# Expert layer: query products in small steps between the sums, the first head's first 128 tokens alone, the first closing norm later

## The chip, the cores and the metric

The kernel runs on one core of one Trainium2 chip. The metric is device time in microseconds (us) of one execution; less is better.

## The reference, cut to what matters

The reference is a whole network on 256 tokens of width 1024: two mixing layers, a layer with a recurrence and attention, and last a layer of experts. Only the expert layer is touched. For each token it makes queries for 8 heads, scores them against two sets of 128 keys, takes the 16 best pairs, fetches for each pair one row of `u` and one row of `v` from tables of 16,384 rows, and adds up 128 rows of `v` per token, each with a coefficient:

```python
def one_chunk(xt):
    q = (xt @ w_q).reshape(BLOCK, PEER_HEADS, PEER_QDIM)
    s1 = jnp.einsum('chd,nd->chn', q[..., :half], keys1).astype(jnp.float32)
    s2 = jnp.einsum('chd,nd->chn', q[..., half:], keys2).astype(jnp.float32)
    t1, i1 = lax.top_k(s1, PEER_TOPK)
    t2, i2 = lax.top_k(s2, PEER_TOPK)
...
    ts, sel = lax.top_k(cand, PEER_TOPK)
    idx = jnp.take_along_axis(cidx, sel, axis=-1)
    g = jax.nn.softmax(ts, axis=-1)
    act = jax.nn.gelu(jnp.einsum('chkd,cd->chk', u[idx], xt))
    coef = (g * act.astype(jnp.float32)).astype(xt.dtype)
    return jnp.einsum('chk,chkd->cd', coef, v[idx])
```

The sum is added to the residual `h`, and a closing RMS norm with a gain gives the output.

## The kernel before

The last stage, `layer_d` (L1382), works in 16 units: 2 tiles of 128 tokens (`tt`) by 8 heads (`h`), the 8 heads of tile 0 first. A unit has 16 gathers. A gather (L1511) is one indirect DMA that POOL issues: for each of 128 tokens one row of `uv`, 8 KB with `u` and `v` side by side, 1 MB in all, into one of 9 slots of a ring (`RING`). Two other users take a slot of the ring: `sq`, the squares for the norm, ahead of the first gather, and `o`, the output tile of a closing norm.

What a unit needs before its gathers:

- `queries(h)` (L1426): for all 256 tokens, 16 matmuls of 128x128 weights by 256 columns (8 pieces `k` of the model width, 2 halves `f`) into one PSUM bank `pq`. An fp32 matmul has two records in the trace, called pieces here.
- `scores(h)` (L1438): ACT copies `pq` to `q`, 4 matmuls of 128 columns (`psc`) multiply with the keys, and ACT copies the scores of tile 0 (`sc0`, two buffers) and of tile 1 (`later`).
- `select(tt, h)` (L1465): on DVE, the 16 best of each key set and then of their pairs (MAX8, FIND_INDEX8 and MATCH_REPLACE8 in the trace), and the row numbers `idx` (L1500), for which POOL waits. It is a generator, so that its steps can be written between experts.

What happens to a gathered row is `expert` (L1514): a product sum on DVE with the normed token rows `xtok` (L1518, `dots`), GELU, coefficient and a diagonal matrix `dg` on ACT (L1521 to L1524), and two matmuls of 512 columns on PE that add `dg` times `v` to `acc[tt]` in PSUM (L1526). Experts run 7 gathers behind (`AHEAD`), and a gather waits until the expert 9 before it has left its slot.

`residual(tt)` (L1408) puts the residual into `acc[tt]` with 8 small matmuls, `token_rows(tt)` (L1450) makes `xtok` from it on DVE, and `close(tt)` (L1530) does the closing norm: a square with sum on ACT (L1534), mean on DVE (L1535), the power -1/2 on POOL (`fy`, L1536), two multiplies on DVE (L1539) and two DMAs of 256 KB from SP (L1540).

The order on each engine is made by a scheduler from the order in which the code stands and from which inputs are ready; each engine then runs its list strictly in order. `tc.issue_after(last)` ties the instructions of a block on one engine behind a given instruction of that engine. Before the change it is used for the steps of `select` only, with the `dots` instruction of the last expert. `queries(i + 1)` and `scores(i + 1)` stand at the head of unit `i`, untied. In front of the gathers stands, for head 0, the product of all 256 tokens and then `rms_cols` (`pst`), which sums the squares `sq` that ACT and POOL prepare.

Of the kernel before, what the change touches and what calls it, by code (L numbers as in the profile page):

```python
# [11 lines left out]
F32 = mybir.dt.float32  # L12
# [4 lines left out]
AF = mybir.ActivationFunctionType  # L17
# [4 lines left out]
P = 128  # L22
D = 1024
KT = D // P
T = 256
# [105 lines left out]
def rms_cols(g, pool, pst, squares, tiles, tag):  # L131

    nc = g.nc
    for i, sq in enumerate(squares):
        token_sums(nc, pst, g.ones, sq, tiles, i == 0, i == len(squares) - 1)
    m, y = (pool.tile([P, len(tiles)], F32, tag=tag + u, name=u) for u in ("ms", "rs"))
    whole = sum(nt == P for _, nt in tiles)
    nc.vector.tensor_scalar(m[:, 0:whole], pst[:, 0:whole], 1.0 / D, 1e-6, ALU.mult, ALU.add)
    for j in range(whole, len(tiles)):
        nt = tiles[j][1]  # L140
        nc.vector.memset(m[:, j:j + 1], 1.0)
        nc.vector.tensor_scalar(m[0:nt, j:j + 1], pst[0:nt, j:j + 1], 1.0 / D, 1e-6, ALU.mult, ALU.add)
    nc.gpsimd.tensor_tensor(y, m, g.mhalf[:, 0:1].to_broadcast([P, len(tiles)]), ALU.pow)
    return y
# [1215 lines left out]
NK = 128  # L1360
PH = 8
TOPK = 16
# [19 lines left out]
def layer_d(g, a, ht, wpools):  # L1382
    tc, nc, g.ahead = g.tc, g.nc, 0
    V, S, G, PE = nc.vector, nc.scalar, nc.gpsimd, nc.tensor
    xt = ht[:, :, META:]
    with ExitStack() as ctx:
# [19 lines left out]
        acc = [pv.tile([P, D], F32, name=f"acc{tt}") for tt in range(2)]  # L1406

        def residual(tt):  # L1408

            for k in range(KT):  # L1410
                PE.matmul(acc[tt][:, k * P:(k + 1) * P], xt[:, k, tt * P:(tt + 1) * P], g.ident, start=(k % 4 == 0),
                          stop=False, skip_group_check=True)

        pf = ctx.enter_context(tc.tile_pool(name="d_f", bufs=1, reuse_waits="tile"))
        later = pf.tile([P, PH, 2, NK], F32, name="sc1")
        sc = {}
        xg = pf.tile([P, KT, T], F32, name="xg")
# [5 lines left out]
            if k:  # L1423
                G.tensor_add(sq[:, k:k + 2, :], sq[:, k:k + 2, :], sq[:, k - 2:k, :])

        def queries(h):  # L1426
            w = g.wq[h]
            p = ps.tile([P, 512], F32, tag="mm", name="pq")
            for k in range(KT):
                for f in range(2):  # L1430
                    PE.matmul(p[:, f * T:(f + 1) * T], w[k // 4][:, k % 4, f * P:(f + 1) * P], xg[:, k, :],  # L1431
                              start=(k == f == 0), stop=(k == KT - 1), skip_group_check=True)
            return p

        ahead = [queries(0)]
        rs = rms_cols(g, px, ps.tile([P, 512], F32, tag="sm", name="pst"), [sq[:, k, :] for k in (KT - 2, KT - 1)], TILES, "d")

        def scores(h):  # L1438
            q = pf.tile([P, 2, T], F32, tag="q", name="q", bufs=2)
            S.activation(q, ahead.pop(0).rearrange("p (f t) -> p f t", f=2), AF.Copy)  # L1440
            p = ps.tile([P, 512], F32, tag="sm", name="psc")
            for tt in range(2):
                for f in range(2):
                    o = (tt * 2 + f) * NK
                    PE.matmul(p[:, o:o + NK], q[:, f, tt * P:(tt + 1) * P], kys[:, f, :], start=True, stop=True)
            sc[0, h], sc[1, h] = pf.tile([P, 2, NK], F32, tag="sc0", name="sc0", bufs=2), later[:, h]
            for tt in range(2):
                S.activation(sc[tt, h].rearrange("p f n -> p (f n)"), p[:, tt * 2 * NK:(tt + 1) * 2 * NK], AF.Copy)

        def token_rows(tt):  # L1450

            for j in range(2):
                js = slice(j * 512, (j + 1) * 512)
                V.tensor_mul(xtok[tt][:, js], acc[tt][:, js], gain["norm2_b"][:, js])
# [54 lines left out]
        def gather(b, s):  # L1509
            r = ring.tile([P, 2 * D], F32, tag="uv", name="uv")  # L1510
            G.indirect_dma_start(r, None, a["uv"], bass.IndirectOffsetOnAxis(ap=b.idx[:, s:s + 1], axis=0))  # L1511
            return r

        def expert(b, s, r):  # L1514

            junk = pk.tile([P, D], F32, tag="junk", name="junk", bufs=1)
            d = dots[:, b.tt, b.h, s:s + 1]
            done = V.tensor_tensor_reduce(out=junk, in0=r[:, 0:D], in1=xtok[b.tt], scale=1.0, scalar=0.0,  # L1518
                                          op0=ALU.mult, op1=ALU.add, accum_out=d)
            gl, cf = (pk.tile([P, 1], F32, tag=u, name=u, bufs=4) for u in ("gl", "cf"))  # L1520
            S.activation(gl, d, AF.Gelu_apprx_tanh, scale=rs[:, b.tt:b.tt + 1])  # L1521
            S.activation(cf, gl, AF.Copy, scale=b.e[:, s:s + 1])  # L1522
            dg = pk.tile([P, P], F32, tag="dg", name="dg", bufs=3)
            S.activation(dg, g.ident, AF.Copy, scale=cf)  # L1524
            for j in range(2):
                PE.matmul(acc[b.tt][:, j * 512:(j + 1) * 512], dg, r[:, D + j * 512:D + (j + 1) * 512], start=False,  # L1526
                          stop=(b.h == PH - 1 and s == TOPK - 1), skip_group_check=True)
            return done.ins

        def close(tt):  # L1530

# [11 lines left out]
        scores(0)  # L1543
        waiting, last = [], None
        for i, (tt, h) in enumerate(order):
            b = Ctx()
            b.tt, b.h = tt, h
            if i == 0:
                for _ in select(tt, h, b):
                    pass  # L1550
                residual(0)
                token_rows(0)
            else:
                for _ in nxt[1]:
                    pass
                b = nxt[0]
            if i + 1 < len(order):
                n = Ctx()
                n.tt, n.h = order[i + 1]
                if i + 1 < PH:  # L1560
                    ahead.append(queries(i + 1))
                    scores(i + 1)
                nxt = n, select(n.tt, n.h, n)
                if i == 2:
                    residual(1)
                    token_rows(1)
            for s in range(TOPK):
                waiting.append((b, s, gather(b, s)))
                if s % 3 == 0 and nxt:
                    with tc.issue_after(last) if last else nullcontext():  # L1570
                        next(nxt[1], None)
                if len(waiting) > AHEAD:
                    last = expert(*waiting.pop(0))
            if i == PH:
                close(0)
        for w in waiting:
            expert(*w)
# [180 lines left out]
```

## Time and profile before

| | us |
|---|---|
| median of 3 runs | 1391.04 |
| lowest and highest | 1388.09 and 1393.73 |
| the profiled execution | 1389.13 |
| its span (first to last instruction) | 1387.2 |
| outside the span | 1.93 |

PE was granted 0.982 of full speed over the span. The chain that ended last, followed back from the end, is 36% PE, 32% DMA, 11% DVE, 10% issue time, 5% ACT and 4% POOL; the DMA part is almost all gathers (30%). Times in the rows further down are us from the start of the span. In the table of stretches, the columns are busy time of each engine with its count of instructions, the granted clock, the busy share of the 16 DMA engines, and what they moved. The expert layer fills the second half: its first gather is issued at 712.73 us.

### The profile page before, as it was taken

To read this page: it belongs to the slowest core of one execution; us is meant where nothing else is said; L and a number is where in the kernel's file an instruction comes from. 1 tells how busy PE (TensorE), PEld (TensorE's weight loads), DVE (VectorE), ACT (ScalarE), POOL (GpSimd) and SP (SyncE) were. 2 spreads that over 40 slices of the span, in tenths; PEclk is the share of its full clock that TensorE was granted. 3 is DMA by queue.
4 is the path that set the end of the run, shared out by engine and by line. 5 is a ranking of instruction groups with operands and counts; after the bars stand their busy time and mean duration, and the time that the engine had idled before them with its cause. 6 is when DMAs were issued, how large, how long until landed. Compare 5 with 4: busy or idle time off the path is not lost.

```text
span 1387.2 us, 18959 instructions
## 1 busy us (share of the span) xinstructions
PE 1232.9 (89%) x6566; PEld 848.1 (61%) x6566; DVE 884.4 (64%) x2103; ACT 664.2 (48%) x1554; POOL 392.3 (28%) x387
## 2 busy tenths in 40 slices
PE   8999997999999899999999998778887778777776
PEld 7778786899998899999976653223222222222222
DVE  6276626676666878666666656766676666666644
ACT  1254522556564686555333455544444444444433
POOL 1001046211114300000043345344443444344430
PEclk9999999999999999999999999999999899999999
DMA  6411311354426354335769999999999899999996
GB/s 233 162 63 61 100 32 39 114 176 131 136 94 204 115 182 142 105 127 188 229 242 420 387 350 422 419 420 420 421 419 419 348 420 420 420 420 420 420 420 248
DMA packets 69727, 364.23 MB, mean 263 GB/s; under 512 B 8752, under 2 KB 14320, under 8 KB 36864
## 3 DMA queue, kind: packets, MB, share of 16 engines
q0 software_dynamic: 36864, 268.45, 47.2%
q1 hardware_dynamic: 32768, 94.56, 21.0%
q8 instruction: 53, 0.87, 0.3%
q14 instruction: 42, 0.34, 0.1%
HBM read 361.94 MB, written 1.05 MB: 262 GB/s over the span
## 4 chain that ended last, share of the span: by engine, by line
PE 36%; DMA 32%; DVE 11%; issue 10%; ACT 5%; POOL 4%; POOLq 0%; SPq 0%; DVEq 0%; ACTq 0%
DMA uv<-in_uv,idx 30%; PE pj L105 5%; PE c_mm L105 5%; PE acc L1526 4%; DVE junk L1518 3%; DVE wl L69 2%; POOL uv L1511 2%; PE pt L313 2%; PE pf L313 2%; PE por L828 2%; PE pf L105 1%; PE pp L614 1%; PE m_mm L105 1%; PE por L105 1%; PE pS L940 1%
## 5 line engine op out<-in xcount | busy, mean ns | idle before, releaser
L1526 PE MATMUL acc<-uv,dg 128*128 128x512 f32 x1024 | 503.6, 622 | 117.7 <-ACT dg L1524 114.1
L1518 DVE CUSTOM_DVE_ANT_0 junk<-uv,xtok 128x1024 f32<-128x1024 f32 x256 | 312.8, 1222 | 208.3 <-DMA uv<-in_uv,idx 207.8
L1526 PEld LDWEIGHTS acc<-uv,dg 128*128 128x128 f32 x1024 | 181.8, 192 | 421.6 <-ACT dg L1524 275.8
L1511 POOL DMA_INDIRECT uv<-in_uv,idx x256 | 273.8, 1070 | 366.0 <-PE acc L1526 265.9
L1521 ACT ACTIVATE gl<-dots,rs 128x1 f32<-128x1 f32 x256 | 75.1, 293 | 296.8 <-DVE dots L1518 296.5
L68 ACT ACTIVATE wh<-raw 128x1024 fp32r<-128x1024 f32 (+2 forms) x124 | 125.8, 1028 | 78.0 <-PE c_mm L105 24.7
L69 DVE TENSOR_TENSOR wl<-raw,wh 128x1024 fp32r<-128x1024 f32 (+3 forms) x115 | 138.2, 1215 | 27.4 <-ACT wh L68 27.0
L1524 ACT ACTIVATE dg<-ident,cf 128x128 f32<-128x128 f32 x256 | 102.5, 400 | 17.2 <-PE acc L1526 9.5
L1522 ACT ACTIVATE cf<-gl,ex 128x1 f32<-128x1 f32 x256 | 75.1, 293 | 7.8
L105 PE MATMUL c_mm<-xgh,wl 128*128 128x256 f32 (+2 forms) x232 | 69.2, 298 | 1.7 <-DVE wl L69 1.7
L105 PE MATMUL c_mm<-xgh,wh 128*128 128x256 f32 (+2 forms) x232 | 68.2, 294 | 1.6 <-DVE xp L1097 1.3
L105 PE MATMUL pj<-wh,xih 128*128 128x256 f32 x240 | 69.4, 289 | 0.0
L105 PE MATMUL pj<-wh,xil 128*128 128x256 f32 x240 | 68.8, 286 | 0.4 <-DVE xil L806 0.4
L105 PE MATMUL pj<-wl,xih 128*128 128x256 f32 x240 | 67.6, 282 | 0.3 <-DVE wl L69 0.3
L105 PE MATMUL c_mm<-xgl,wh 128*128 128x256 f32 (+2 forms) x232 | 67.6, 291 | 0.0
L313 PE MATMUL pt<-wp,xm 128*128 128x256 f32 x256 | 62.3, 389 | 0.0
L1431 PE MATMUL pq<-xg,wq 128*128 128x256 f32 x256 | 60.2, 379 | 0.0
L1431 PEld LDWEIGHTS pq<-xg,wq 128*128 128x128 f32 x256 | 48.0, 190 | 15.6 <-issue 10.5
L313 PEld LDWEIGHTS pt<-wp,xm 128*128 128x128 f32 x256 | 46.3, 190 | 7.3 <-issue 0.3
L105 PEld LDWEIGHTS pj<-wh,xih 128*128 128x128 f32 x240 | 45.2, 188 | 3.7 <-issue 3.3
L105 PEld LDWEIGHTS c_mm<-xgh,wl 128*128 128x128 f32 (+1 forms) x232 | 44.1, 190 | 3.2 <-DVE wl L69 2.9
L105 PEld LDWEIGHTS c_mm<-xgh,wh 128*128 128x128 f32 (+1 forms) x232 | 44.1, 190 | 2.5 <-issue 1.5
(449 smaller groups left out, 2331.8 us busy)
## 6 DMA issues: line engine op xcount, KB each, us to landing
wq<-in_wd_q SPq DMA_DIRECT2D x16, 512.0 KB, 6.9
wp<-in_wa_k SPq DMA_DIRECT2D x8, 512.0 KB, 9.5
raw<-in_wa_o SPq DMA_DIRECT2D x8, 512.0 KB, 3.9
wp<-in_wa_r SPq DMA_DIRECT2D x8, 512.0 KB, 4.8
wp<-in_wa_v SPq DMA_DIRECT2D x8, 512.0 KB, 4.4
wp<-in_wa_g SPq DMA_DIRECT2D x8, 512.0 KB, 4.3
raw<-in_wb_k SPq DMA_DIRECT2D x8, 512.0 KB, 3.9
raw<-in_wb_q SPq DMA_DIRECT2D x8, 512.0 KB, 4.0
```

The source lines that it names most:

```text
L68: nc.scalar.activation(xh, x, AF.Copy)
L69: return (engine or nc.vector).tensor_sub(xl, x, xh.bitcast(F32)).ins
L105: last = nc.tensor.matmul(out, s, m, start=(k == n == 0), stop=(k == kt - 1 and n == len(ops) - 1))
L313: PE.matmul(out, s, m, start=(k == 0), stop=(k == KT - 1))
L828: last = nc.tensor.matmul(out, m, v, start=(k == n == 0 and fresh), stop=(k == KT - 1 and n == 2), skip_group_check=True)
L1431: PE.matmul(p[:, f * T:(f + 1) * T], w[k // 4][:, k % 4, f * P:(f + 1) * P], xg[:, k, :], start=(k == f == 0), stop=(k == KT - 1), skip_gr ...
L1511: G.indirect_dma_start(r, None, a["uv"], bass.IndirectOffsetOnAxis(ap=b.idx[:, s:s + 1], axis=0))
L1518: done = V.tensor_tensor_reduce(out=junk, in0=r[:, 0:D], in1=xtok[b.tt], scale=1.0, scalar=0.0, op0=ALU.mult, op1=ALU.add, accum_out=d)
L1521: S.activation(gl, d, AF.Gelu_apprx_tanh, scale=rs[:, b.tt:b.tt + 1])
L1522: S.activation(cf, gl, AF.Copy, scale=b.e[:, s:s + 1])
L1524: S.activation(dg, g.ident, AF.Copy, scale=cf)
L1526: PE.matmul(acc[b.tt][:, j * 512:(j + 1) * 512], dg, r[:, D + j * 512:D + (j + 1) * 512], start=False, stop=(b.h == PH - 1 and s == TOPK - ...
```

## The change

`queries` becomes a generator that yields after each of the 8 pieces `k`, and can take half of the tokens. Its steps, 2 matmuls each, are asked for at every second gather, two heads ahead of the unit that needs them, and tied on PE behind the matmuls of the expert before (`behind(1)`; `expert` now returns these too). `scores` follows at the end of the unit. Ahead of the first gather only the queries and scores of the first 128 tokens of head 0 are made; head 1, the residual, the token rows and the other 128 tokens of head 0 come after `select` of unit 0. `sc0` has three buffers in place of two. `residual(1)` stands ahead of the gathers of unit 1 (before: unit 2). `close(0)` stands at the end of unit 11 (before: unit 8).

```diff
-        def queries(h):
-            w = g.wq[h]
-            p = ps.tile([P, 512], F32, tag="mm", name="pq")
+        def queries(h, to, tiles=slice(0, T)):
+
+            w, n = g.wq[h], tiles.stop - tiles.start
+            to.append(ps.tile([P, 512], F32, tag="mm", name="pq"))
+            p = to[-1]
             for k in range(KT):
                 for f in range(2):
...
-            return p
-
-        ahead = [queries(0)]
+                yield
+
+        ahead = []
+        for _ in queries(0, ahead, slice(0, P)):
+            pass
...
-            return done.ins
+            return done.ins, summed.ins
...
+        def behind(i):
+
+            return tc.issue_after(last[i]) if last else nullcontext()
+
+        scores(0, (0,))
+        for _ in units[0].steps:
+            pass
+        for h, tiles in ((1, slice(0, T)), (0, slice(P, T))):
+            for _ in queries(h, ahead, tiles):
+                pass
+            if h:
                 residual(0)
                 token_rows(0)
...
+                scores(1)
+        scores(0, (1,))
+        for i, b in enumerate(units):
+            then = units[i + 1] if i + 1 < len(units) else None
+            asked = queries(i + 2, ahead) if i + 2 < PH else iter(())
+            for _ in b.steps:
+                pass
+            if i == 1:
+                residual(1)
+                token_rows(1)
             for s in range(TOPK):
                 waiting.append((b, s, gather(b, s)))
-                if s % 3 == 0 and nxt:
-                    with tc.issue_after(last) if last else nullcontext():
-                        next(nxt[1], None)
+                if s % 3 == 0 and then:
+                    with behind(0):
+                        next(then.steps, None)
+                if s % 2:
+                    with behind(1):
+                        next(asked, None)
                 if len(waiting) > AHEAD:
                     last = expert(*waiting.pop(0))
-            if i == PH:
+            if i + 2 < PH:
+                for _ in asked:
+                    pass
+                with behind(1):
+                    scores(i + 2)
+            if i == PH + 3:
                 close(0)
```

What the change makes of the engines' lists, at three places. First PE ahead of the first gather, before (`pq` are queries, `pst` the sums of squares, `acc` from `ident` the residual, `psc` scores):

```order
L1431 MATMUL pq<-xg,wq 128x256 x16
L127 MATMUL pst<-ones,sq 128x1 x4
L1411 MATMUL acc_7240<-ident,ht 128x128 x3
L1445 MATMUL psc<-kys,q 128x128 x4
L1411 MATMUL acc_7240<-ident,ht 128x128 x5
L1431 MATMUL pq<-xg,wq 128x256 x18
```

and after:

```order
L1433 MATMUL pq<-xg,wq 128x128 x16
L127 MATMUL pst<-ones,sq 128x1 x4
L1433 MATMUL pq<-xg,wq 128x256
L1450 MATMUL psc<-kys,q 128x128 x2
L1433 MATMUL pq<-xg,wq 128x256 x15
L1411 MATMUL acc_7240<-ident,ht 128x128 x8
L1450 MATMUL psc<-kys,q 128x128 x4
```

The first queries have half the columns, two score matmuls follow the sums of squares after one other matmul, and the residual has moved behind them. On DVE, in the same place, the list before has the token rows inside the first selection:

```order
L1483 CAST ivf<-iv 128x32
L1454 TENSOR_TENSOR xtok_7237<-acc_7240,norm_b 128x512
L1458 MAX ts<-cand 128x8
L1454 TENSOR_TENSOR xtok_7237<-acc_7240,norm_b 128x512
L1459 MAX_INDEX se<-ts,cand 128x8
```

and after, behind the row numbers of unit 0:

```order
L1501 TENSOR_TENSOR eq<-eq,ivf 128x512
L1503 TENSOR_REDUCE ix<-eq 128x32
L1505 SCALAR_TENSOR_TENSOR idx<-ix 128x16
L1459 TENSOR_TENSOR xtok_7237<-acc_7240,norm_b 128x512 x2
L1463 MAX tv<-sc_7381 128x8 x2
```

Both multiplies of `token_rows(0)` now stand after `idx`. Second, PE among the experts of units 1 and 2 (two `acc` matmuls are one expert), before:

```order
L1526 MATMUL acc_7240<-uv,dg 128x512 x2
L1431 MATMUL pq<-xg,wq 128x256 x3
L1526 MATMUL acc_7240<-uv,dg 128x512 x2
L1431 MATMUL pq<-xg,wq 128x256 x4
L1526 MATMUL acc_7240<-uv,dg 128x512 x2
L1431 MATMUL pq<-xg,wq 128x256 x3
```

and after:

```order
L1450 MATMUL psc<-kys,q 128x128 x4
L1531 MATMUL acc_7240<-uv,dg 128x512 x2
L1433 MATMUL pq<-xg,wq 128x256 x2
L1531 MATMUL acc_7240<-uv,dg 128x512 x4
L1433 MATMUL pq<-xg,wq 128x256 x2
L1531 MATMUL acc_7240<-uv,dg 128x512 x4
```

Before, the last query matmul stands ahead of expert 30 (of 256, counted from 0), with three or four between two experts; after, it is two for every two experts, up to expert 88. Third, POOL around the first closing norm, as one piece of the difference:

```order
-L1511 DMA uv<-in_uv,idx 128x2048 x144
-L1536 TENSOR_TENSOR fy_9678<-fm_9677,mhalf 128x1
-L1511 DMA uv<-in_uv,idx 128x2048 x112
-L1536 TENSOR_TENSOR fy_11409<-fm_11408,mhalf 128x1
+L1516 DMA uv<-in_uv,idx 128x2048 x192
+L1541 TENSOR_TENSOR fy_10427<-fm_10426,mhalf 128x1
+L1516 DMA uv<-in_uv,idx 128x2048 x64
+L1541 TENSOR_TENSOR fy_11429<-fm_11428,mhalf 128x1
```

and ACT there, after the change (the `gl` ahead of the square is the one of expert 189; before the change it is the one of expert 141):

```order
L1526 ACTIVATE gl<-dots,rs 128x1
L1539 ACTIVATE o,fss_10425<-acc_7240 128x1024
L1527 ACTIVATE cf<-gl,ex 128x1
L1529 ACTIVATE dg<-ident,cf 128x128
L1526 ACTIVATE gl<-dots,rs 128x1
```

The closing norm has moved by 48 gathers; `fy` still stands directly behind the last gather of a unit on POOL, and the square on ACT behind the GELU of the expert two before that gather.

## Rows read from the trace of the kernel before

**Rows 1.** The page's first line: span and instructions.

```profile
span 1387.2 us, 18959 instructions
```

**Rows 2.** Stretches of the expert layer: busy by engine, clock, DMA share, GB/s.

```profile
720.00:780.00 60.00, 57.72 (x216) 36.68 (x215) 40.66 (x109) 28.22 (x78) 23.00 (x22) 1.00 1.01 418
780.00:832.00 52.00, 51.31 (x162) 29.51 (x163) 30.38 (x84) 24.18 (x75) 21.77 (x21) 1.00 0.96 352
832.00:1070.00 238.00, 190.48 (x385) 67.74 (x384) 160.54 (x428) 113.52 (x318) 104.93 (x97) 0.98 1.01 420
1070.00:1100.00 30.00, 20.31 (x40) 7.27 (x40) 18.54 (x56) 10.82 (x33) 10.68 (x10) 0.94 0.84 335
```

**Rows 3.** Gathers, answer on line L1511: time from issue to landing.

```profile
DMA to landing us min/median/max: 5.7/17.4/18.4
```

**Rows 4.** Timeline, PE and POOL among units 1 and 8: start, duration, instruction, idle before.

```profile
756.28 1.88 PE L1526 MATMUL acc<-uv,dg 128*128 128x512 f32 x4
757.99 1.46 PE L1431 MATMUL pq<-xg,wq 128*128 128x256 f32 x6
759.29 1.88 PE L1526 MATMUL acc<-uv,dg 128*128 128x512 f32 x4
...
1070.35 0.94 POOL L1511 DMA_INDIRECT uv<-in_uv,idx  x1 [1.56 <-PE acc L1526]
```

**Rows 5.** Timeline ahead of the first gather, all engines.

```profile
693.59 6.78 PEld L1431 LDWEIGHTS pq<-xg,wq 128*128 128x128 f32 x32
693.71 7.07 PE L1431 MATMUL pq<-xg,wq 128*128 128x256 f32 x32
...
695.02 3.99 POOL L1424 TENSOR_TENSOR sq<-sq 128x512 f32<-128x512 f32 x3 [12.16 <-ACT sq L1422]
...
700.61 0.95 PE L127 MATMUL pst<-ones,sq 128*128 128x1 f32 x8
700.81 0.60 ACT L1440 ACTIVATE q<-pq 128x512 f32<-128x512 f32 x1 [4.83 <-PE pq L1431]
...
702.17 1.06 PE L1445 MATMUL psc<-kys,q 128*128 128x128 f32 x8
...
703.07 1.28 PE L1411 MATMUL acc<-ident,ht 128*128 128x128 f32 x10
703.27 0.66 ACT L1448 ACTIVATE sc<-psc 128x256 f32<-128x256 f32 x2 [1.86 <-PE psc L1445]
703.68 0.49 DVE L1458 MAX8 tv<-sc 128x8 f32<-128x128 f32 x2 [1.92 <-ACT sc L1448]
```

**Rows 6.** The same timeline later: selection of unit 0 and first gather.

```profile
706.18 0.21 DVE L1477 TENSOR_TENSOR cand<-tv 128x64 f32<-128x64 f32 x1
...
706.39 0.68 DVE L1454 TENSOR_TENSOR xtok<-acc,norm_b 128x512 f32<-128x512 f32 x1
706.99 0.27 DVE L1458 MAX8 ts<-cand 128x8 f32<-128x112 f32 x1
...
707.76 0.08 DVE L1459 MATCH_VALUE_LOAD se<-ts,cand 128x8 f32 x1
...
712.73 1.20 POOL L1511 DMA_INDIRECT uv<-in_uv,idx  x1 [10.19 <-DVE idx L1500]
```

**Rows 7.** Timeline, the first closing norm on ACT and POOL.

```profile
1084.45 0.29 ACT L1521 ACTIVATE gl<-dots,rs 128x1 f32<-128x1 f32 x1 [1.22 <-DVE dots L1518]
1084.74 1.02 ACT L1534 ACTIVATE o<-acc 128x1024 f32<-128x1024 f32 x1
...
1086.13 1.54 POOL L1536 TENSOR_TENSOR fy<-fm,mhalf 128x1 f32<-128x1 f32 x1 [14.84 <-DVE fm L1535]
```

**Rows 8.** Two stretches after it, columns as in rows 2.

```profile
1090.00:1100.00 10.00, 4.86 (x8) 1.85 (x8) 4.52 (x16) 2.37 (x8) 6.37 (x7) 0.81 0.94 388
1100.00:1110.00 10.00, 8.93 (x15) 3.35 (x14) 7.57 (x18) 7.14 (x18) 5.46 (x5) 0.68 1.01 424
```

**Rows 9.** PE alone in that stretch.

```profile
1097.49 3.78 PE L1526 MATMUL acc<-uv,dg 128*128 128x512 f32 x4 [3.31 <-ACT cf L1522]
```

More of the change, by code (lines that the diff above doesn't have):

```diff
@@ L1424, in layer_d @@
                 G.tensor_add(sq[:, k:k + 2, :], sq[:, k:k + 2, :], sq[:, k - 2:k, :])
-        def queries(h):
-            w = g.wq[h]
-            p = ps.tile([P, 512], F32, tag="mm", name="pq")
+        def queries(h, to, tiles=slice(0, T)):
+            w, n = g.wq[h], tiles.stop - tiles.start
+            to.append(ps.tile([P, 512], F32, tag="mm", name="pq"))
+            p = to[-1]
             for k in range(KT):
                 for f in range(2):
-                    PE.matmul(p[:, f * T:(f + 1) * T], w[k // 4][:, k % 4, f * P:(f + 1) * P], xg[:, k, :],
+                    PE.matmul(p[:, f * n:(f + 1) * n], w[k // 4][:, k % 4, f * P:(f + 1) * P], xg[:, k, tiles],
@@ L1432, in queries, with scores @@
                               start=(k == f == 0), stop=(k == KT - 1), skip_group_check=True)
-            return p
-        ahead = [queries(0)]
+                yield
+        ahead = []
+        for _ in queries(0, ahead, slice(0, P)):
+            pass
         rs = rms_cols(g, px, ps.tile([P, 512], F32, tag="sm", name="pst"), [sq[:, k, :] for k in (KT - 2, KT - 1)], TILES, "d")
-        def scores(h):
-            q = pf.tile([P, 2, T], F32, tag="q", name="q", bufs=2)
-            S.activation(q, ahead.pop(0).rearrange("p (f t) -> p f t", f=2), AF.Copy)
+        def scores(h, tiles=(0, 1)):
+            n = P * len(tiles)
+            q = pf.tile([P, 2, T], F32, tag="q", name="q", bufs=2)[:, :, 0:n]
+            S.activation(q, ahead.pop(0)[:, 0:2 * n].rearrange("p (f t) -> p f t", f=2), AF.Copy)
@@ L1441, in scores @@
             p = ps.tile([P, 512], F32, tag="sm", name="psc")
-            for tt in range(2):
+            for j in range(len(tiles)):
                 for f in range(2):
[L1444 to L1448, printed above, removed]
+                    o = (j * 2 + f) * NK
+                    PE.matmul(p[:, o:o + NK], q[:, f, j * P:(j + 1) * P], kys[:, f, :], start=True, stop=True)
@@ L1450, in token_rows @@
+            for j, tt in enumerate(tiles):
+                sc[tt, h] = later[:, h] if tt else pf.tile([P, 2, NK], F32, tag="sc0", name="sc0", bufs=3)
+                S.activation(sc[tt, h].rearrange("p f n -> p (f n)"), p[:, j * 2 * NK:(j + 1) * 2 * NK], AF.Copy)
         def token_rows(tt):
@@ L1525, in expert @@
             for j in range(2):
-                PE.matmul(acc[b.tt][:, j * 512:(j + 1) * 512], dg, r[:, D + j * 512:D + (j + 1) * 512], start=False,
-                          stop=(b.h == PH - 1 and s == TOPK - 1), skip_group_check=True)
-            return done.ins
+                summed = PE.matmul(acc[b.tt][:, j * 512:(j + 1) * 512], dg, r[:, D + j * 512:D + (j + 1) * 512],
+                                   start=False, stop=(b.h == PH - 1 and s == TOPK - 1), skip_group_check=True)
+            return done.ins, summed.ins
         def close(tt):
@@ L1542, in layer_d @@
         order = [(tt, h) for tt in range(2) for h in range(PH)]
-        scores(0)
+        units = [Ctx() for _ in order]
+        for b, (b.tt, b.h) in zip(units, order):
+            b.steps = select(b.tt, b.h, b)
         waiting, last = [], None
[L1545 to L1550, printed above, removed]
+        def behind(i):
+            return tc.issue_after(last[i]) if last else nullcontext()
@@ L1551, in layer_d @@
+        scores(0, (0,))
[5 more added lines that the diff above has]
+            if h:
                 residual(0)
                 token_rows(0)
[L1553 to L1566, printed above, removed]
+                scores(1)
```

## Prediction

> **What bounds the kernel now.** I read the page first, then the expert layer by stretches, then the timelines at the three places that the change touches. The profiled execution has a span of 1387.2 us [rows 1]; its own time is 1389.13 us, 1.9 below the median of the runs shown (1391.04). The sum is made against the first and then set on the second.
>
> The reader should look at the last number of each stretch in [rows 2]. From 832 to 1070 us the gathers move 420 GB/s with the DMA engines fully busy while PE is busy for 190 of 238 us: the DMA engines are the bound there. A gather is 128 rows of 8 KB, 1.049 MB, so it takes 2.50 us at that rate, and 16 of them, a unit, 39.9 us. The bound holds only while enough gathers are queued, and there are two places where it fails. From 780 to 832 us the rate is 352 GB/s while PE is busy for 51.3 of 52 us: PE is the bound. From 1070 to 1100 us it is 335 GB/s, around the first closing norm. Ahead of all this the chain runs through PE and DVE alone, until the first gather is issued at 712.73 [rows 6]. What is gained up to the first gather, or in a stretch where the rate falls below 420, moves the end; anything else on PE, DVE or ACT is hidden behind the gathers.
>
> Why PE is the bound in the second stretch is seen in [rows 4]: an expert's four pieces start at 756.28, six query pieces at 757.99, the next expert at 759.29. So an expert takes 1.71 us, a query piece 1.30 / 6 = 0.217, and the pitch is 3.01 us, 0.51 more than the gathers' 2.50. Since a landing takes 17.4 us after issue in the median [rows 3], some 7 gathers are on their way and the deficit shows late: the rate holds at 418 GB/s from 720 to 780 [rows 2] and falls after that.
>
> **The change part by part.**
>
> *Queries in steps.* The list on PE now has four query pieces for two experts: 2 x 1.71 + 4 x 0.217 = 4.29 us against 5.0 us for two gathers. Over a unit, PE needs 16 x 1.71 + 32 x 0.217 + 8 score pieces at 0.11 (below) = 35.2 of 39.9 us. PE is no longer the bound, so the stretch at 352 GB/s should run at 420: 52 x (420 - 352) / 420 = 8.4 us. The bounds are 0, if another wait takes its place, and 8.7, if the 2 GB/s missing from 720 to 780 come back too. I take 8.4, because the stretch from 832 on has the same experts and selections without queries and runs at 420. The new waits lie behind this: once in a unit ACT's copy of the queries to `q` stands ahead of an expert's `dg`, and waits for the last step on PE. Behind it are queued that expert's and the following coefficients on ACT, for which PE's sums wait, for which POOL's next gather waits. It costs at most a step and a copy, 4 x 0.217 + 0.60 [rows 5] = 1.5 us in a unit that has 4.7 us to spare on PE, with 17.4 us of gathers queued. Nothing.
>
> *Head 0's first 128 tokens.* In [rows 5] 32 query pieces of 256 columns start at 693.71 and end as `pst` starts at 700.61, 0.216 each. Pieces of 128 columns are seen in the scores: 8 in 703.07 - 702.17 = 0.90 us, 0.11 each. So the half product ends near 693.7 + 32 x 0.11 = 697.3. But `pst` stands next in PE's list, and its squares are ready only when POOL's last addition ends, 695.02 + 3.99 = 699.01. That is what is late next. With 0.2 us for the first weights `pst` starts at 699.2, and takes 0.8 as before (700.61 until the residual, 0.95 with its tail); one query matmul follows, 0.43; then four score pieces, whose tail ends 3 x 0.11 + 0.28 = 0.6 after their start: 701.1. ACT's copy of the scores started 0.04 after the tail of eight (702.17 + 1.06), at 703.27, so it now starts at 701.1: 2.1 us gained. Bounds: 0.8, if halving the columns gave nothing and only the shorter list behind `pst` counted (700.61 + 1.9 = 702.5); 4.1, if the squares were no bound (POOL's spans are rough) and the 3.4 us of the halves came on top. I take 2.1, the row of the addition. The DVE wait for the scores and the rest of the chain follow unchanged.
>
> At this place a rule of the Trainium skill speaks against the change. The row shows 32 weight loads within the same 6.8 us as 32 matmul pieces, and pieces of half the columns at half the pitch [rows 5]. "TensorE: Matmul & The Clock Gate", section "The mechanism", says that a weight load overlaps matmuls in flight only where the row groups differ. By that rule loads of full width could not hide, half the columns would not give half the time, and this part would be worth its lower end and the forecast 1.3 us later. The trace disagrees.
>
> *Token rows behind `idx`.* Before, the first multiply of `xtok` starts at 706.39, just when the candidates are complete (706.18 + 0.21), and the lookup that needs the first MAX8 starts at 707.76 [rows 6]. Without both multiplies MAX8 starts at 706.4 and its result, 0.27 later, lets the lookup start near 706.7: 1.0 us gained. Bounds: 0.7, one multiply, and 1.4, both. The multiplies move into the gap between issue and first landing (at least 5.7 us [rows 3]); the residual that they need is done 15 x 2 x 0.217 + 16 x 0.11 = 8.3 us after the scores of unit 0 have begun at 700.5, near 708.8, when `idx` is about due. So the first product sum doesn't wait. The first gather goes out near 712.7 - 3.1 = 709.6.
>
> *Second half of head 0, residual and token rows of tile 1, third `sc0` buffer.* They stay on PE, DVE and ACT, between the first gather and the first landed rows or among experts with time to spare: 16 x 0.11 + 2 x 0.68 us, once. Nothing; without the gathers queued ahead it would cost 3 us.
>
> *The closing norm four units later.* [Rows 7] and the last POOL row of [rows 4] show the stall: POOL issues a gather at 1070.35, then comes `fy`, which waits 14.8 us, until ACT's square at 1084.74 has followed the GELU at 1084.45. That GELU is of the expert two before the last issued gather, so it waits for rows still under way, and the next gather on POOL stands behind `fy`. The stretch loses 30 x (420 - 335) / 420 = 6.1 us. All its instructions, ACT's square, DVE's mean and multiplies, POOL's power and SP's two DMAs, move together by 48 gathers; on POOL and ACT they stand to their neighbours as before, only SP has nothing queued there. So the stall stays, at another time: 0. Bounds: -6.1, gone; +1, for a different meeting with a selection on DVE.
>
> **Sum.** 8.4 + 2.1 + 1.0 + 0 = 11.5 us. Profiled execution: 1389.1 - 11.5 = 1377.6 (span 1375.7). Against the median: 1391.0 - 11.5 = 1379.5.
>
> **The rivals.**
>
> *The starving stays in part.* ACT and PE now hand over more often, and if each hand-over cost what I hid, half of 8.4 would be left: 1379.5 + 4.2 = 1383.7, or up to 1386 with the start at its lower end. For it speaks that each engine keeps its list's order; against it the 4.7 us to spare.
>
> *The first gather comes no earlier*, because something that the trace of before hides gates the selection: 1391.0 - 8.4 = 1382.6. Against it: every row from the scores to the gather follows its predecessor at once.
>
> *The closing norm's stall vanishes:* 1379.5 - 6.1 = 1373.4. This is also the question whether that part does what its place suggests; the lists say that nothing about the wait changed.
>
> *Slower: PE at its lower clock among the experts.* After 3.31 us without work an expert took 3.78 us [rows 9], twice the 1.88 among the queries [rows 4], so the clock stood at its lower level, 1.2 GHz; the granted clock was 0.81 and 0.68 in two stretches of 10 us [rows 8], so the episode cost 1.9 + 3.2 = 5.1 us of PE's work. The steps now leave PE short idle times where it was busy without a break. One episode in a unit would be paid by the 4.7 us to spare; two would leave 5.5 us in each of some 7 units, 38 us, of which the queue hides about 10 (before, 0.51 us for each of the 60 / 3.01 = 20 gathers from 720 to 780, until the rate fell): 1379.5 + 28 = 1408. It decides from about 1.5 episodes in each unit. Against it: from 832 to 1070 PE is busy for 80% in the same rhythm at a clock of 0.98 [rows 2], and will be busier here. The Trainium skill, "TensorE: Matmul & The Clock Gate", section "Loop structure matters more than you think", says the same as this rival: matmuls of one product should stay together, not be cut up by waits for DMA, or PE falls to its lower clock. No row here shows that at this load.
>
> **How the numbers follow.** Chances: forecast 0.69; starving in part 0.12; first gather no earlier 0.07; stall gone 0.07; slower 0.05. The range goes from the vanished stall, 1373, to the first rival's far end, 1386; that leaves out the slower case and little of the others. A measurement of this kernel can tell about 0.5% (7 us, 1384) from no change. Faster by more: nearly all of the forecast, the vanished stall, most of the late first gather and a third of the first rival, 0.82; slower 0.05; same 0.13.
>
> **What would show it.** First gather near 709.6 us, the selection starting 2.1 us and the gather 3.1 us earlier; 420 GB/s from about 720 us up to the closing norm, with two-step groups of queries between pairs of experts; POOL waiting some 15 us for `fy` near 1180 us with about 335 GB/s over 30 us; span near 1376. It is wrong if the rate dips below 400 anywhere ahead of the norm, if PE's clock is below 0.9 among units 0 to 6, or if `fy` waits less than 10 us.

## The result, and the profile after

The changed kernel takes 1377.35 us (median of 5 runs, 1376.45 to 1379.71) beside 1390.59 for the kernel before (5 runs): a ratio of 0.9909, 95% interval 0.9891 to 0.9928. It is 0.9% faster, 2.1 us below the forecast of 1379.5. The profiled execution took 1377.35 us, where the sum gave 1377.6; its span was forecast as 1375.7.

```profile
span 1375.4 us, 19008 instructions
```

The 11.8 us between the spans fall into three parts. The first query matmul starts at 692.34 in place of 693.71 [rows 5]: 1.37 us from code that the change doesn't touch, so it isn't counted as the change's; why this start moves from run to run stays open. From there to the issue of the first gather it takes 15.84 us in place of 19.02: 3.18. From that issue to the end of the span it takes 667.2 us in place of 674.5: 7.25. The change is worth the last two, 10.4 us, where 11.5 were forecast.

The stretches of the expert layer, columns as in [rows 2]:

```profile
717.00:780.00 63.00, 57.16 (x171) 29.87 (x171) 42.34 (x108) 32.50 (x89) 29.54 (x27) 1.00 1.01 420
780.00:832.00 52.00, 47.20 (x139) 23.91 (x138) 36.19 (x101) 25.01 (x72) 24.79 (x20) 1.00 1.01 420
832.00:1070.00 238.00, 200.47 (x492) 86.91 (x491) 160.32 (x431) 115.15 (x321) 108.58 (x95) 0.99 1.01 419
...
1178.00:1210.00 32.00, 20.94 (x43) 6.96 (x41) 19.26 (x59) 11.79 (x35) 11.27 (x10) 1.00 0.74 296
```

The second row answers the 352 GB/s of before: 420, with PE busy for 47.2 of 52 us instead of 51.3, at full clock. The stretch with the closing norm is now the one from 1178 on, and still low. PE among the experts of unit 1, against [rows 4]:

```profile
755.50 3.60 PE L1531 MATMUL acc<-uv,dg 128*128 128x512 f32 x8
758.94 1.03 PE L1433 MATMUL pq<-xg,wq 128*128 128x256 f32 x4
759.80 3.96 PE L1531 MATMUL acc<-uv,dg 128*128 128x512 f32 x8
```

Two experts and four query pieces come every 4.3 us (755.50 to 759.80), as worked out, against 5.0 for two gathers. ACT waits less for the queries, not more. From the tables of waits, first before (728 to 832 us), then after (725 to 835); the columns are total, times, longest:

```profile
ACT q L1440 <- PE pq L1431: 30.7, 5, 8.8
ACT q L1445 <- PE pq L1433: 4.3, 3, 2.6
```

The start, against [rows 5] and [rows 6]:

```profile
692.22 3.66 PEld L1433 LDWEIGHTS pq<-xg,wq 128*128 128x128 f32 x32
692.34 3.73 PE L1433 MATMUL pq<-xg,wq 128*128 128x128 f32 x32
693.65 3.98 POOL L1424 TENSOR_TENSOR sq<-sq 128x512 f32<-128x512 f32 x3 [12.17 <-ACT sq L1422]
697.68 1.05 PE L127 MATMUL pst<-ones,sq 128*128 128x1 f32 x8 [1.61 <-POOL sq L1424]
699.11 0.61 PE L1450 MATMUL psc<-kys,q 128*128 128x128 f32 x4
699.75 0.38 ACT L1453 ACTIVATE sc<-psc 128x256 f32<-128x256 f32 x1 [3.26 <-PE psc L1450]
700.16 0.49 DVE L1463 MAX8 tv<-sc 128x8 f32<-128x128 f32 x2 [1.24 <-ACT sc L1453]
...
708.18 1.20 POOL L1516 DMA_INDIRECT uv<-in_uv,idx  x1 [8.47 <-DVE idx L1505]
```

The half product takes 3.73 us instead of 7.07; PE then stands for 1.61 us until POOL's last addition has ended, and `pst` goes ahead of the scores. MAX8 follows the first query matmul by 7.82 us (before 9.97: 2.15 gained), and the gather follows MAX8 by 8.02 us (before 9.05: 1.03 gained). The closing norm, against [rows 7]:

```profile
1194.21 0.29 ACT L1526 ACTIVATE gl<-dots,rs 128x1 f32<-128x1 f32 x1 [1.22 <-DVE dots L1523]
1194.78 1.02 ACT L1539 ACTIVATE o<-acc 128x1024 f32<-128x1024 f32 x1 [0.28 <-issue]
1196.17 1.55 POOL L1541 TENSOR_TENSOR fy<-fm,mhalf 128x1 f32<-128x1 f32 x1 [15.73 <-DVE fm L1540]
1197.91 0.99 POOL L1516 DMA_INDIRECT uv<-in_uv,idx  x1 [0.19 <-issue]
```

The stall is there again, a little longer: `fy` waits 15.7 us, and the next gather goes out behind it.

### The profile page after: what moved, and what is told of

Same layout as the page of the kernel before. It is cut to its first block, busy times and chain, and to the rows that moved or that the text cites. A ratio compares the mean times of both kernels' runs of the same rounds, so it can differ in the third digit from the quotient of the medians.

```text
span 1375.4 us, 19008 instructions
## 1 busy us (share of the span) xinstructions
PE 1226.6 (89%) x6598; PEld 850.7 (62%) x6598; DVE 884.1 (64%) x2103; ACT 667.1 (49%) x1555; POOL 401.0 (29%) x387
## 3 DMA queue, kind: packets, MB, share of 16 engines
q0 software_dynamic: 36864, 268.45, 47.2%
## 4 chain that ended last, share of the span: by engine, by line
PE 39%; DMA 31%; DVE 12%; issue 9%; ACT 5%; POOL 4%; POOLq 0%; SPq 0%; DVEq 0%; ACTq 0%
DMA uv<-in_uv,idx 30%; PE c_mm L105 6%; PE pj L105 5%; PE acc L1531 4%; DVE junk L1523 3%; POOL uv L1516 2%; DVE wl L69 2%; PE pt L313 2%; PE pf L313 2%; PE por L828 2%; PE pf L105 1%; PE pp L614 1%; PE m_mm L105 1%; PE por L105 1%; PE pS L940 1%
## 5 line engine op out<-in xcount | busy, mean ns | idle before, releaser
L1516 POOL DMA_INDIRECT uv<-in_uv,idx x256 | 282.3, 1103 | 347.7 <-PE acc L1531 254.0
L1433 PE MATMUL pq<-xg,wq 128*128 128x256 f32 (+1 forms) x288 | 63.6, 356 | 0.0
L105 PEld LDWEIGHTS pj<-wh,xih 128*128 128x128 f32 x240 | 45.1, 188 | 3.7 <-issue 3.7
```

What stands on the lines that cost most here:

```text
L105: last = nc.tensor.matmul(out, s, m, start=(k == n == 0), stop=(k == kt - 1 and n == len(ops) - 1))
L1433: PE.matmul(p[:, f * n:(f + 1) * n], w[k // 4][:, k % 4, f * P:(f + 1) * P], xg[:, k, tiles], start=(k == f == 0), stop=(k == KT - 1), ski ...
```

## The experiments

The theory: the gathers starve where PE's pitch for an expert (the time from one expert to the next on PE) is longer than a gather's 2.50 us, so the steps remove that; the earlier start counts only where PE is no bound behind it; the closing norm costs the same wherever it stands in this form. The rivals: the whole products at the head of a unit cost by their hand-over to ACT, not by PE's pitch; the parts simply add up; the norm's place matters.

Ahead of the first query matmul no variant changes an instruction, yet it started between 690.33 and 697.86 us. So the variants are compared by two spans of each profile, from the first query matmul to the issue of the first gather (A) and from that to the end of the span (B), beside the median and its ratio to the kernel before on the same chip.

| kernel | median, us | ratio, 95% interval | A, us | B, us |
|---|---|---|---|---|
| before | 1390.59 | | 19.02 | 674.5 |
| changed | 1377.35 | 0.9909 (0.9891 to 0.9928) | 15.84 | 667.2 |
| changed, again | 1379.33 | 0.9919 (0.9898 to 0.9939) | 15.87 | 667.4 |
| start alone | 1388.97 | 0.9998 (0.9981 to 1.0015) | 16.32 | 676.1 |
| steps alone | 1383.27 | 0.9954 (0.9937 to 0.9971) | 18.19 | 667.4 |
| half the queries | 1385.25, one run | | 19.35 | 667.7 |
| queries twice | 1385.82, one run | | 15.86 | 673.0 |
| queries three times | 1424.38, one run | | 15.86 | 712.9 |
| norm at unit 8 | 1377.66, one run | | 16.12 | 667.8 |
| norm at the end | 1379.10 | 0.9924 (0.9908 to 0.9941) | 16.91 | 663.7 |
| norm split | 1377.29 | 0.9896 (0.9879 to 0.9913) | 17.12 | 664.1 |
| square elsewhere | 1379.28, one run | | 16.30 | 664.9 |
| sums late | 1376.48 | 0.9894 (0.9874 to 0.9914) | 14.53 | 667.5 |
| sums late and norm split | 1373.56 | 0.9881 (0.9853 to 0.9909) | 13.64 | 664.8 |

The kernels with the steps, the queries as they are and the first closing norm in its old form ahead of other gathers lie between 667.2 and 667.8 in B. The third buffer of `sc0` and the earlier `residual(1)` were not tried apart.

### The changed kernel again

> The changed kernel, unaltered, timed beside the next ones on their chip, because the part ahead of the expert layer, which no variant touches, moved by several us from run to run (with the closing norm at the end the first query matmul started 6.6 us later than in the changed kernel's profile, with a clock of 0.79 in the stretch from 170 to 190 us). All theories: 1377 to 1379, and 667 us from the issue of the first gather to the end of the span.

1379.33 us, A and B within 0.2 us of the first profile. (With the norm at the end the first query matmul came 5.5 us later than in the changed kernel, 697.86 against 692.34, not 6.6.) The difference of the medians, 2 us, is what such a comparison leaves open.

### The start alone

```diff
-        ahead = [queries(0)]
+        ahead = [queries(0, slice(0, P))]
...
-        scores(0)
+        scores(0, (0,))
```

> The kernel before with the new start alone: head 0's first 128 tokens ahead of the first gather, token rows and everything else of the start behind idx. The later queries stay whole, at the head of a unit and untied, and the closing norm stays at the end of unit 8. Theory: the start moves the first gather 3.2 us earlier against the first query matmul, as in the changed kernel, but PE is the bound up to about 832 us whatever is queued, and since it has the same experts and queries to do the 3.2 us are lost again in the stretch at 352 GB/s: median within 1.2 us of the kernel before. Rival: the parts of the change simply add up: 3.2 us faster, about 1387.4, with the offset of the first product sum kept through to the last.

Not measurably faster: 0.9998. A is 2.7 us shorter, B 1.6 us longer, so 1.1 us is left in the profile. The stretch from 780 to 832 (columns as in [rows 2]):

```profile
780.00:832.00 52.00, 51.49 (x177) 31.54 (x176) 28.86 (x77) 22.06 (x67) 19.98 (x19) 1.00 0.94 344
```

The gathers were ahead, and PE, busy for 51.5 of 52 us, let them starve more: 344 GB/s instead of 352. The parts don't simply add up: the start pays in full only with the steps behind it.

### The steps alone

```diff
-        for _ in queries(0, ahead, slice(0, P)):
+        for _ in queries(0, ahead):
...
-            if i == PH + 3:
+            if i == PH:
                 close(0)
```

> The changed kernel with two of its parts undone: all 256 tokens of head 0 ahead of the first gather, and the closing norm back at the end of unit 8. The queries in steps, two heads ahead, remain. Theory (the steps are worth the stretch at 352 GB/s, and nothing else): 420 GB/s from 780 to 832 us, an offset of the product sums that grows by 7.4 us between the first unit and the fourth, and with the token rows still behind idx and a shorter list behind pst 1 to 2 us from the start: about 1391 - 8.4 = 1382.5. Rival (the steps need the earlier first gather to have enough queued): a dip below 400 GB/s remains somewhere between 720 and 832 and the gain is under 5 us, 1386 or more.

```profile
780.00:832.00 52.00, 45.48 (x135) 23.33 (x134) 33.02 (x88) 24.49 (x69) 24.13 (x21) 1.00 1.01 420
```

The rate is 420 without the earlier start. B is 7.1 us shorter, A 0.8; the median 1383.27 is 0.8 us above the 1382.5 expected. (Beside the kernel before on the same chip, 1389.18, that is 5.9 us; the two spans of the profile give 7.9.) So of the 3.18 us of the start, 0.8 come without the shorter first product. The rest comes with it, and the run above shows that most of it is lost where the steps are missing.

### Less and more work on PE

Half of the query matmuls, otherwise the kernel before (the queries of heads 1 to 7 stay bunched):

```diff
-            for k in range(KT):
+            step = 2 if h else 1
+            for k in range(0, KT, step):
```

> The kernel before with half of the query matmuls of heads 1 to 7 left out (every second piece of the model width, so that these heads select by other queries), the rest still bunched at the head of each unit. Theory (what starves the gathers is the length of the stretch in which PE needs 3.01 us for an expert; half as many pieces leave about 0.51 x 10 = 5 us a unit, and the queue hides about 10): the rate stays at 420 GB/s from 780 to 832 and first gather to end is 667 us, as with the steps, in place of 674.5. Rival (bunches as such, whole products with a hand-over to ACT, starve them): a dip below 400 GB/s remains and 672 us or more.

Every query matmul of heads 2 to 7 twice or three times, otherwise the changed kernel:

```diff
-                for f in range(2):
+                for f in [f for f in range(2) for _ in range(times)]:
```

> As the run with every query matmul of heads 2 to 7 three times, but twice (these heads select by other queries). Theory (PE's pitch against the gathers'): 2 x 1.71 + 8 x 0.217 + 0.11 = 5.27 us for two experts against 5.0: 0.27 x 48 = 13 us too much, of which the queue and PE's single idle gaps hide about 10: 0 to 4 us slower than the changed kernel, 667 to 671 us from first gather to end, where the threefold one had 712.9. Rival (extra work on PE costs in proportion, without a threshold): half of the threefold one's 45 us, about 690.

> The changed kernel with every query matmul of heads 2 to 7 made three times and added up, so that these heads select by other queries: PE gets 8 more query pieces for each two experts, every list keeps its order. Theory (PE's own pitch is what starves the gathers): 2 x 1.71 + 12 x 0.217 + 0.11 = 6.1 us for two experts against 5.0 for two gathers, 48 such pairs, 54 us in all of which the queue hides about 10: 40 to 45 us slower, 1420, with PE busy throughout units 0 to 5 and about 340 GB/s there. Rival (the whole queries at the head of a unit cost the time by the hand-over, ACT waiting for a whole product, and not by PE's pitch): the steps are still spread, so under 10 us slower.

One stretch of each (half, twice, three times), columns as in [rows 2]:

```profile
780.00:832.00 52.00, 42.67 (x93) 15.99 (x92) 34.61 (x90) 24.38 (x70) 21.01 (x21) 0.97 1.01 420
```

```profile
850.00:900.00 50.00, 49.77 (x163) 29.79 (x162) 34.11 (x88) 25.06 (x72) 22.62 (x19) 1.00 0.99 398
```

```profile
850.00:900.00 50.00, 50.00 (x172) 31.84 (x171) 26.54 (x73) 19.10 (x57) 17.43 (x16) 1.00 0.95 345
```

Bunched as before but half as long, the products starve nothing: B is 667.7, and the rate is 420 where it was 352. This run alone can't tell PE's work from the hand-over, since ACT's wait for the queries falls too, to 13.0 us (728 to 832). Spread out but longer, they do, at the rate that PE's pitch gives: 2 x 1.049 MB in 5.27 us is 398 GB/s, and in 6.13 us 342; the rows show 398 and 345. ACT's wait for the queries doesn't follow the loss (twice, 725 to 960 us; three times, 725 to 1000):

```profile
ACT q L1448 <- PE pq L1435: 35.5, 6, 6.4
ACT q L1448 <- PE pq L1435: 11.9, 6, 2.1
```

With twice the queries it is 35.5 us, more than in the kernel before, and 5.8 us are lost (673.0 - 667.2); with three times it is 11.9, and 45.7 are lost. So it is PE's work against the gathers' time, not the hand-over. The loss has a threshold: twice the queries are 13 us too much by the pitch, and lose 5.8, a little over the 0 to 4 expected; three times are 54 too much, and lose 45.7. The queue hides some 7 and 9 us, not 10.

### The place of the closing norm

```diff
-            if i == PH + 3:
+            if i == PH:
                 close(0)
```

> The changed kernel with the closing norm of the first tile back at the end of unit 8 in place of unit 11. Theory (the stall moves with the norm and costs about the same): POOL waits 14 to 16 us for fy near 1060, the same 48 product sums around it take 4 to 5 us more than 48 without it, and the time is within 1 us of the changed kernel's 1377.4. Rival (the later place is worth something, for instance because unit 8 has more beside it): 3 us or more slower, above 1380.

```profile
1058.48 0.94 POOL L1516 DMA_INDIRECT uv<-in_uv,idx  x1 [2.53 <-PE acc L1531]
...
1074.26 1.54 POOL L1541 TENSOR_TENSOR fy<-fm,mhalf 128x1 f32<-128x1 f32 x1 [14.84 <-DVE fm L1540]
```

The same wait at another time, the same B within 0.6 us: the three units (48 gathers) are worth next to nothing. Then behind the last gather:

```diff
-            if i == PH + 3:
+            if i == len(order) - 1:
                 close(0)
```

> The changed kernel with the closing norm of the first tile behind the last gather of all in place of behind unit 11's. Theory (what the norm costs is that POOL's list stops at fy while gathers stand behind it): with no gather behind it the 4 to 5 us of the stall go, 1377.4 - 4.5 = about 1373, and the offsets of the product sums show no step at 188 to 208. A part could come back at the end if the norm's own work on ACT and DVE meets the last experts: at most its 1.0 us square and two multiplies, 2 us. Rival (the cost is the norm's own work, the slot of the ring that its output takes, or its DMA): the cost moves with it and the time stays at 1377.

```profile
1348.27 0.94 POOL L1516 DMA_INDIRECT uv<-in_uv,idx  x1 [1.57 <-PE acc L1531]
1364.03 1.54 POOL L1541 TENSOR_TENSOR fy<-fm,mhalf 128x1 f32<-128x1 f32 x1 [14.82 <-DVE fm L1540]
```

`fy` waits as long, but no gather stands behind it. B falls by 3.5 us. The product sums 188 and 208 (counted from 0) are written, in the changed kernel and then in this one, at:

```profile
1191.82 0.08 DVE L1523 DVE_READ_ACCUMULATOR2_ANT dots<- 128x1 f32 x1
1247.55 0.08 DVE L1523 DVE_READ_ACCUMULATOR2_ANT dots<- 128x1 f32 x1
...
1198.41 0.08 DVE L1523 DVE_READ_ACCUMULATOR2_ANT dots<- 128x1 f32 x1
1249.05 0.08 DVE L1523 DVE_READ_ACCUMULATOR2_ANT dots<- 128x1 f32 x1
```

These 20 take 50.6 us, where they took 55.7 in the changed kernel, and 1.6 of the 5.1 us come back in the last units. The median, 1379.1, doesn't show the gain. In the profiled run (1380.5) the first query matmul came 5.5 us later and A was 1.1 longer than in the changed kernel, so there it is the part ahead that hides it; the other runs have no trace.

### What the closing norm waits for

The square writes into a slot of the ring (`o`). First the norm taken apart, with the square in `xtok` of tile 0, which is no longer needed, and the power 8 gathers later:

```diff
-            o = ring.tile([P, 2 * D], F32, tag="uv", name="o")[:, 0:D]
-            S.activation(o, acc[tt], AF.Square, accum_out=ss)
+            S.activation(xtok[tt], acc[tt], AF.Square, accum_out=ss)
             V.tensor_scalar(m, ss, 1.0 / D, 1e-6, ALU.mult, ALU.add)
+            yield
+            o = ring.tile([P, 2 * D], F32, tag="uv", name="o")[:, 0:D]
...
+                if (i, s) == (PH + 4, 7):
+                    next(closing, None)
```

> The changed kernel with the first tile's closing norm taken apart: the square writes into the token rows of tile 0, which are no longer needed, in place of a slot of the ring, and the power, the multiplies and the output follow behind the 8th gather of unit 12 in place of behind the last of unit 11. Nothing is left out. Theory (the cost is POOL's list standing at fy while the square waits for a slot of the ring): fy waits for nothing, the step of 5.1 us in the product sums from 188 to 208 goes, first gather to end 667.2 - 5.1 = 662 us, time about 1372.5. Rival (the norm's own work costs the time): 667 us from the first gather to the end, as in the changed kernel.

```profile
1202.10 1.09 POOL L1542 TENSOR_TENSOR fy<-fm,mhalf 128x1 f32<-128x1 f32 x1
...
1230.12 0.94 POOL L1516 DMA_INDIRECT uv<-in_uv,idx  x1 [8.09 <-DMA out_dram<-o]
```

`fy` waits for nothing. B is 664.1, 3.2 us less than the changed kernel, not 5.1: the gather that takes the output's slot next waits 8.1 us for the output's DMA, and the 20 product sums take 51.8 us, 1.2 more than without a norm there. The other 0.7 shows in unit 14, which is that much longer in every kernel without the stall at unit 11; why stays open. Then the square alone, with `fy` in its old place:

```diff
-            o = ring.tile([P, 2 * D], F32, tag="uv", name="o")[:, 0:D]
-            S.activation(o, acc[tt], AF.Square, accum_out=ss)
+            S.activation(xtok[tt], acc[tt], AF.Square, accum_out=ss)
...
+            o = ring.tile([P, 2 * D], F32, tag="uv", name="o")[:, 0:D]
```

> The changed kernel with one half of the split alone: the square of the closing norm writes into the token rows of tile 0, not into a slot of the ring; power, multiplies and output stay behind the last gather of unit 11. Theory A (the square waits for the slot of the ring, and fy for the square): the square moves up to the end of unit 7 in ACT's list, fy finds its input ready, the stall goes as with the split, 664 us from first gather to end. Theory B (fy's place behind the last gather is what costs, whatever the square does): fy or what follows it still holds POOL by 10 us or more, 667 us.

```profile
1045.45 1.02 ACT L1538 ACTIVATE xtok<-acc 128x1024 f32<-128x1024 f32 x1 [2.07 <-PE acc L1531]
...
1185.25 0.59 POOL L1540 TENSOR_TENSOR fy<-fm,mhalf 128x1 f32<-128x1 f32 x1
```

The square has moved up by 150 us, to the end of tile 0, and `fy`, still directly behind unit 11's last gather, waits for nothing. B is 664.9. So what held POOL was the slot: the tile `o` comes out of the ring behind the 192nd gather, and that put the square late in ACT's list.

### What binds the start

```diff
-        rs = rms_cols(g, px, ps.tile([P, 512], F32, tag="sm", name="pst"), ...
...
         scores(0, (0,))
+        rs = rms_cols(g, px, ps.tile([P, 512], F32, tag="sm", name="pst"), ...
```

> The changed kernel with the sums of squares (pst) behind the scores of head 0's first 128 tokens on PE, not ahead of them. Nothing is left out. Theory (what binds the start is that pst waits for POOL's last addition, and the scores stand behind it in PE's list): the scores follow the queries at once, PE waits 1 to 2 us less ahead of them, the selection starts 2 to 2.5 us earlier against the first query matmul, and first gather and end move with it: 1377.4 - 2.3 = about 1375. Rival (ACT's copies or DVE's chain bind, or ACT's copy of the queries is late): the first gather stays within 0.5 us of the changed kernel's 15.4 us after the first query matmul.

```profile
695.40 0.38 ACT L1452 ACTIVATE sc<-psc 128x256 f32<-128x256 f32 x1 [0.93 <-PE psc L1449]
...
696.77 0.16 DVE L138 TENSOR_SCALAR ms<-pst 128x2 f32<-128x2 f32 x1 [4.96 <-PE pst L127]
696.85 0.48 DVE L1462 MAX8 tv<-sc 128x8 f32<-128x128 f32 x2
```

The 15.4 us in the expectation was read from a row that the window had cut; the whole row gives 15.84. A is 14.53, so 1.3 us were gained and not 2 to 2.5. The scores are copied 5.07 us after the first query matmul in place of 7.41, so `pst` was the bind on PE. But on DVE the mean `ms` stands ahead of MAX8 and waits for the same `pst`: MAX8 starts 1.45 us after the copy, where it was 0.41. The wait has moved from one list to another.

The last version takes that away too, and has the split norm:

```diff
+        next(units[0].steps)
+        next(units[0].steps)
+        with tc.issue_after(first[1]):
+            rs = rms_cols(g, px, ps.tile([P, 512], F32, tag="sm", name="pst"), ...
```

> The changed kernel with the split closing norm of the earlier run, and with the sums of squares behind the first head's scores on PE and, on DVE, the mean of them (ms) inside the first selection in place of ahead of it. Nothing is left out. In the run with pst moved alone the scores were copied 1.9 us earlier, but MAX8 started 1.45 us after the copy in place of 0.41, since ms stood ahead of it on DVE and waited for pst. Theory: with ms behind the first MAX8s the first gather comes 13.5 us after the first query matmul (15.4 in the changed kernel, 14.5 with pst moved alone), and first gather to end stays at the split norm's 664 us: 1377.4 - 1.9 - 3.2 = about 1372.5 if the part ahead is as in the changed kernel's profile, up to 1375 if it is as in the repeat of it. Rival (something else holds the first gather): 14.5 us again, about 1375.

```profile
699.20 1.05 PE L127 MATMUL pst<-ones,sq 128*128 128x1 f32 x8 [0.31 <-POOL sq L1424]
699.34 0.48 DVE L1464 MAX8 tv<-sc 128x8 f32<-128x128 f32 x2 [4.02 <-ACT sc L1452]
...
701.43 0.14 DVE L138 TENSOR_SCALAR ms<-pst 128x2 f32<-128x2 f32 x1
...
707.48 1.20 POOL L1517 DMA_INDIRECT uv<-in_uv,idx  x1 [5.12 <-DVE idx L1506]
```

MAX8 now starts while `pst` runs. A is 13.64, B 664.8: 4.6 us less than the changed kernel in the two together. The median is 1373.56, the lowest of all, 3.8 and 5.8 us under the two medians of the changed kernel, but those weren't taken beside it and the intervals of the ratios overlap: by the medians it is not shown to be faster than the changed kernel.

## Why the prediction was right, step by step

- **The bound.** Right: behind the first gather the rate counts, and PE's pitch sets it where it is longer than a gather's time. The pitch gave the rate to 3 GB/s in both kernels with more queries.
- **Queries in steps, 8.4.** Right in kind, 1.2 too large: 7.1 in the run with the steps alone, 7.25 in the changed kernel. The lost rate itself was read rightly. In the first 119 us from the first gather the changed kernel moved 48.9 MB, the kernel before 45.1, and 3.74 MB are 8.9 us. The product sums show where the lead then shrinks: it is 8.8 us at the 48th, 1.0 goes in unit 3 and 0.5 in unit 5, for a reason that stays open, 0.85 goes to the longer stall of the norm (20 product sums over the stall take 54.9 us before and 55.7 after, 50.6 without one), and 0.7 comes back in unit 14.
- **Head 0's first 128 tokens, 2.1.** 2.15, for the reason given: PE waits for POOL's last addition, and `pst` starts 5.34 us after the first query matmul (5.5 forecast). Moving `pst` behind the scores confirmed it. The 32 full-width weight loads (3.66 us) hide behind the 3.73 us of half-width pieces. That goes against the sentence of the Trainium skill that was weighed ("TensorE: Matmul & The Clock Gate", section "The mechanism"): in this trace they overlap. What the step left unsaid is that most of these microseconds are lost without the steps behind them.
- **Token rows behind `idx`, 1.0.** 1.03.
- **The closing norm, 0.** Right that the stall only moves, by 48 gathers, which are three units and not the four of the prediction's heading (15.7 us, 296 GB/s over 32 us; forecast some 15 and 335 over 30). Its size, 6.1, was too large: by the product sums 4.2 before and 5.1 after, and 2.3 to 3.5 us of B come back when it goes. The prediction named the GELU two experts back as what the square waits for; the slot of the ring put the square there. POOL's list behind `fy` is strict: the gather goes 0.19 us after it. The Trainium skill says so of this engine's queue ("PSUM — Partial Sum Buffer", section "Engine vs sequencer instructions"), and the trace agrees.
- **The rivals.** The hand-over to ACT fell from 30.7 to 4.3 us of waits. That this wait costs little was shown above by the run with twice the queries. The first gather came 3.18 us earlier against the first query matmul, so nothing hidden gated the selection. PE's clock was 1.00 from 717 to 832 us with the steps cut up among the gathers, so the slower case did not come.
- **The total.** 10.4 us from the change against 11.5, and 1.4 us from an earlier first query matmul, which no step held. That the profiled time agrees to 0.2 us is partly luck. The medians of five runs each differ by 13.2 us, 1.7 more than forecast; without traces of all runs that can't be divided between the change and the part ahead.

## What to carry to other kernels

Work that is moved out of a bunch pays where the bunch made one engine's pitch longer than the transfer's time, and the new pitch tells the rate; the queue in front hid some 7 and 9 us here, at 13 and 54 us of excess. An earlier start is worth little while another engine is the bound behind it (1.1 of 2.7 us here), so try such edits together as well as alone. A wait in an engine's list is removed at its source: ask which buffer put the instruction there, and look for the next list that waits for the same value.

## What the runs showed of the hardware

PE's new wait of 1.61 us ahead of `pst` had a price that comes and goes. Nine profiles of kernels have this wait. In seven of them the granted clock fell soon after it, 5.9 to 7.6 us after the first query matmul, from full speed to its lower level of 1.2 GHz; in two (the changed kernel, queries twice) it stayed at 1.00. What counts is when. The four score pieces start 6.8 us after the first query matmul. In five profiles the fall came ahead of them or among them: they take 0.88 to 1.06 us, and A is 16.12 to 17.12. In the other two (the changed kernel again, queries three times) it came at their end or behind it: they take 0.61 us, and A is 15.86 and 15.87, as without a fall. The granted clock with the start alone (two rows), and in the changed kernel again (columns as in [rows 2]):

```profile
696.00:700.00 4.00, 2.39 (x17) 2.14 (x17) 0.16 (x1) 0.38 (x1) 2.54 (x3) 0.93 0.96 322
700.00:704.00 4.00, 4.00 (x15) 3.33 (x15) 3.01 (x20) 0.38 (x1) 0.08 (x1) 0.64 0.41 167
...
700.00:704.00 4.00, 4.00 (x20) 3.42 (x20) 2.02 (x14) 0.38 (x1) 0.71 (x1) 0.70 0.65 240
```

The cost was 0.3 to 1.3 us of A where the fall met the scores. In the five profiles without this wait (before, the steps alone and half the queries with none, the two kernels with `pst` behind the scores with 0.31 us) the clock stayed at 1.00 there, and the pieces took 0.61. Why it fell in seven of the nine and not in the other two stays open.
